# One hybrid decoder block on one core: other loads, roots and order in the first stage

## The chip, the cores and the metric

The kernel runs on one core of a Trainium2 chip. TensorE multiplies and transposes, VectorE and ScalarE do elementwise work, GpSimd (POOL) and SyncE (SP) here only issue DMAs. The metric is the device time in microseconds of one execution of the whole program, the median of several runs. Data begin and end in device memory.

## The reference, cut to what matters

One decoder layer for 512 tokens of width 1024. A conditioning vector `c` gives six modulation vectors; the input is normalized, modulated, and projected; two groups of heads (a gated delta rule, and a native sparse attention) work on the projection, an output projection and a gated MLP with a short convolution follow.

```python
mod = jax.nn.silu(c) @ ada_w + ada_b
shift1, scale1, gate1, shift2, scale2, gate2 = jnp.split(mod[:, None, :], 6, axis=-1)
h = rmsnorm(x, norm1_w) * (1 + scale1) + shift1
proj = h @ w_in
... # gated delta heads and sparse attention heads on proj -> mixed
x = x + gate1 * (mixed @ w_out)
h2 = rmsnorm(x, norm2_w) * (1 + scale2) + shift2
up = causal_dwconv(h2 @ ffn_w_up, ffn_conv_w, ffn_conv_b)
a, b = jnp.split(up, 2, axis=-1)
x = x + gate2 * ((jax.nn.silu(a) * b) @ ffn_w_down)
```

Here `rmsnorm(x, w) = x * rsqrt(mean(x*x) + 1e-6) * w`. All inputs are float32.

## The kernel before, in words

**Arithmetic.** A float32 product is made of three products of rounded parts (`mm3`): every operand is split into `hi` (rounded, by ScalarE or VectorE) and `lo = src - hi` (VectorE), and `hi*hi`, `hi*lo`, `lo*hi` are accumulated in a PSUM bank. So each weight tile costs one rounding and one subtraction before TensorE can use it.

**First stage.** `x` is loaded as eight tiles of 128 tokens by 512 features (256 KB each), `xs[t][j]`. For each token block `t`, both halves are squared and summed (`square2`, on ScalarE or VectorE), `rsqrt1` makes the reciprocal root on VectorE, and `scale` multiplies the tiles by it. The root starts from a bit trick and refines it in three steps of two operations each; `rsqrt` is the same for several columns, with three operations in each step.

The width of 1024 is worked through in eight steps `k` of 128 features. Step `k` needs
- the modulation of its 128 features: `mod_scale(k, 0, ...)` and `mod_shift(k, 1)`. For most of them two tiles of `ada_w` (`adat`, 128 x 512, 256 KB) are loaded and VectorE reduces each against `cb`, the row of `silu(c)` broadcast over all partitions (`mod`, a `scalar_tensor_tensor` with `accum_out`). `cb` is made by eight TensorE products of `sc = silu(c)` with the identity. Only the scale of `k = 0` is made otherwise: from `adat0`, by eight products of one column on TensorE;
- the transposes of the four `xs` columns (TensorE, with `ident`), `Identity` with scale and bias on ScalarE into `h`, and the split of `h` into `hTh[k]`, `hTl[k]`;
- the weights `wg0[k]` (128 x 896, 448 KB) and their split.

Then 7 x 3 products go into seven PSUM banks `g0` (`g0_first` for `k = 0`, in two halves of 256 columns; `g0_mm` for the others, 512 columns).

**Warm-up.** At the start TensorE is given `IDLE = 64` products of a blank tile (`128x256`), sect "warm"; nothing uses them. ScalarE is given one Silu of a blank column.

**Later stages.** Seven projections in this first pass, then convolutions, the delta rule in four chunks of tokens, the sparse attention, the output projection, a second norm (`norm2`, with `rsqrt1`), the up-projection by a seven-product scheme, and the down-projection. `rsqrt` is called for the norm of k and q (32 columns), and through `rms` in the four scans, for `nq`, `kv` and `cmp`.

**What sets the order.** Every operation is recorded into a plan and then emitted in an order that is written out as packed text: `ORDER` holds the differences of operation numbers, `CHOICE` says for each operation that ScalarE or VectorE could do which of the two does it. Each engine does its instructions in the order of emission, and so does each DMA queue. Since the plan emits everything from one place, all instructions have the same line, L262, in the profile.

DMAs are issued by SP (hardware queue), some by GpSimd (software queue). Before the first real product SP issues, in this order: x[0,0], x[0,1], x[1,1], x[1,0], ident, x[2,0], x[3,1], x[3,0], x[2,1], shift k=0 (second half), `adat0` (first half), `wg0[0]`, `adat0` (second half), shift k=0 (first half), then tiles for k = 1 and 2. GpSimd loads the first 48 columns of the parameters `pt` (`c`, norm weights, modulation biases).

TensorE's first instructions are: 29 fillers; the eight products for `cb`; then the other 35 fillers, one to seven at a time, between the transposes for k = 0, 1, 2 and the eight products for the scale of k = 0; then the 42 products of `g0_first`.

Of the kernel before, what the change touches and what calls it, by code (L numbers as in the profile page):

```python
# [12 lines left out]
IDLE = 64  # L13
F32R = mybir.dt.float32r
I32 = mybir.dt.int32
AF = mybir.ActivationFunctionType
# [5 lines left out]
P = 128  # L22
# [12 lines left out]

GQ, GK, GV, GZ = 0, 512, 1024, 1536
# [9 lines left out]
def _fill(table, fields):  # L46
    at = 0
    for name, n in fields:
# [7 lines left out]
                   ("alog", 4), ("dtb", 4), ("w2k", 128), ("w2v", 128)])  # L56
NCST = _fill(CST, [("triu", 128), ("ones", 128), ("negT", 128), ("neg", 128), ("eye2", 512), ("lv", 2 * 128),
# [5 lines left out]
c-ozNcbF8#7wx@0Gn-gg1PPLJ1_>fTa?VJWAUPvBD@l?l8Ob@S2#A0Z6iE^U6a++amaydDF1tI^_r6m#1H$`$@1MthGt*sNU0rqS+;h*ZYNF^)cuWFQBqfG7  # L63
N!XxGi7ASn>sRWb59o>hq5=Jol9Xwkw!v>WMNp!qrdzrJW&eMFxkJC(RJ9(Z!BI-OU|UOu&u_1_JAe|<ht!k-eR`}1aqTEg*RNlz)09lV&F8AR`ZnFw=Q@@K
Xma}Z<>!hPp$B^0-q(drpez%4Fuvq;1|J{BzY*6O<NLplhwf=lI-vVCKb^(Z?Br?~WkU;3RP>%c(p|6gV=z9I=tq5~wP-W!6hi^6PpeVGiz~}*&7oABe$v|X
2d?L(E%;7{r<kWXcve~pqi~G#n&zbK7>!>qs$X-X>;~@kQ8bQDY7Tsxc`$#;@Qgn-FOJI4JlvIrp6XRtsSQd*PwIR4J{_uS{tDpEWc0Uf&GhOQ?S$t&*C-qh
(n)xJyq-e+Y^Zxyv!FB$J=8>f0~QS6u5$FJcBJ{}>3OY0SF`{u;iCM$W~F~%lVrd~tiFYI%xI5k4SYY-Cwdz-O-XXPj9xOXUqu^JXt2hssgaHHV@?=X(_+4j
h40{w9J+?e;`ydVG1%!3U@|p&P=<bnz1~3|0~$lY-k-<Jc<ghd(B}x0-T`V#(mu3!OW(w}BPkzU0)}EWAD)qeZllH%{RlHu0Bu$ygZLU2mGyB~0Xn5+QJ<+9
uz61_((mZ&8?cWLcTS+WdKpM#%#o>6-{SWlJIA&8n*5`M(PkK3Q}0WBq=NNtqQ*5Xh5p5apG$~DkIj|d_#KTaqv%`u(U&igG3L~${n)m*B&=EDEzO7-JENu8
FQ)8*j-f2DVPn(?S~mE74(B<^%)(Hd&9jz6?XWzF0gQD;So_5ExH>8<SJE%KTp#FD%*JKSY&|}LTGQuL(vHKAe#gR&Yjluy3tOJpo(9qz8cT)sB!#Jmztgsu  # L70
oxezdiZq&m4jXLgX<({|e!*4Y*YD~kZ_Yq2ji&Wsd$d$yWy*|sn8JQ<@1%GY@o+)?8-2{KS7`$k@~q?Z{w{h<+5$C2FxI8&b0R(K{k6HGObu(BC|UydKc%C-
?ujw*mCV$IPXM7MsFQrb4($cjr%1W5J&C>fg7;Zcq_3|351k`ZdAy9%%2bzrz$|W|k8~fuD+Q?@SE1dSLo0>VPHfJTr6xU6<4?)a_EjKkwtmj*q*vJD#FgF+
flRbQ9_l-^9+)V{F}|lsc_;_P$sRqd4LJwRk!Jj@T)~X@2s@D2f-eIpm$W*KlW-cv`@C=aSIb&0i5dNvQ_)yS2Hbe4EFYJ&bW|Jh_fiheuF2m>0`9!3*L4)1
1UF8XOz`ORoD=h#0KSR#txdeC=_w;$l=V8CZ%VPSZHe!29w6ej+{C>Kd}iY^;JOQXPBJ@<ou&Rf9H+%KANP~FVevXKu>^}YpxfRI{!{SPqrhrB=CPt4@wrL2
# [12 lines left out]
u1f_`J<5$}lq}*Y+Lxa23fDvBCEW452e>R+`3VsrH%G&7t4Kx4>|ArFdj<rIHp}c(lJ45Z^G)C$rGht=qhB@BTRN~0-Z73x$x+W6lsn)DYZS%V0mN?6Ce9;w
vge&Z1u&0lBO0iMoxjnS!p=mUB>VJ$r(D2ClfZSgXqZ&wL$Lh&Gy)Osu;-fQ3Va7#`M{Yz+QK!(Xw6OB2nZ~J=zfwq=|tz5OcbN%R5y6kU5IPuNe^|pb4MD>
c_+VH&Uxxa&=77WMRDz8{MJOwUnoB#3YeT>hekN7v^nnF#J|E1_sNGq&{nVwL#^}#lWx*FxcVzvJS_b=8wK2NxDA+fAWcJ^L3p0(HfZdA)SI(Oewysmcau9A
i3L%C6R4KEmn+L&Rw(u?VwCX5P!mk|_%2wyvMh8uxei^zy?=9gF=KfETn%s{;im)L^`0gH)y|$<vd2x-i<}2ssL(crJ*xwS5gAWuLB#xDxr2U6Z_q4i1Py&3  # L90
sEDLyati$`962wcyu@*|Z01s^e+h9qnFO_D_s9kDw>YCjI$>lm65&+UZDL}-YM7JgMmW#i^?2q;8RE3kx5aUCU`$Cm2$=9W0nK3Bsl(ePAD@xbxXa{13Un0V
Q&NbpB2sMQOVUKA>2&m`A6JCxO^5h(iR(*k^rIcL%E!C`a~w(ibhw_Uyqcd6%SbTx+rac(8m5ad(<!JT?ShRzL&=En!-+BOG}tpcqGzOZ=R&kne&qwmnW{mn
pFpfUuQ!lw{jFc~b6qGYk$p|p*>r$rxleT$SCzV+t$_pFSG({e-K-sf)w$^Xd-6M%5OU6IK1t;yxn?B4!>e-2Wj1=YE~%Rc?>J`FZAFykMaE#X@?|yINB}uk
F7(>fLU?vGa<_emXIW_vdRB&7(E~XP+-&5Q93iKvC{OpcO)#D-oC!L-zpr>wektl4(9*~jdO&ICgkAmxQ+x26fLTc)shz!AL;eI$^rdRr3K*;4Iqp8Ax9MXY
s44j@lz|8S5w7>8lttz$egw<^gS_D>tdbuX@k<1!;f+#M-$E?kOZ8yuqH-Q6%BrimAXwvfEvfO8&#4c+v4tGDB)8?$@FfY|JhSy)pscsPZVuG*{1OPTM=oe@
k3+Kp88NH3z))?%a|94kba3EHPw7B3m(<^>uQMS~+DXz_x2xwTssn2W^s=mWM|c|0@IY11C*Z{*G~3_L`zMqXQzoZ1r=^mC3f|E=4Ez;vw|gQeoj#!Qfiq58
V9rHMi=aV>)Y<e7b)y*BL8;sV-UY}-ys*Y;;K{EW;obFRAm)1!mksRqc&TjQj;9Kp@fYwm1?O}F>SLTzwAg>pvl1<y<a~ix9S84hOJBI7Jj>-GxHJcPGa)e4
f$HNrR887C2eqDlE9cz8j)$(mZ?bwTB5%2?(*r5J@nHXG>B^r3(s^ruDQ5*HdKOqeNuYayEKUQ=M;dvqP)u%irxwj|b2}~{^EYr(LCr-&0bSK++*Hm(4bG8#
# [1347 lines left out]
```

## Time and profile before

| | |
|---|---|
| median of 3 runs | 653.7 us (653.41 to 654.44) |
| the profiled execution: its own time | 654.27 us |
| its span, first to last instruction | 652.4 us |
| instructions | 12661 |
| TensorE products busy | 647.6 us |
| TensorE weight loads busy | 584.1 us |
| VectorE busy | 613.4 us |
| ScalarE busy | 467.9 us |
| moved by DMA | 132.44 MB |

In rows of the profile PE is TensorE's products, PEld its weight loads, DVE VectorE, ACT ScalarE, SPq the DMA issues of SP. Tiles are named by their class: S, R, s and C are SBUF pools (512 columns, 1024 columns, small, kept), P is PSUM; `in_adat_dram` stands for both `adat` and `adat0`, `in_wg_dram` for `wg0`. Times in a timeline are start and duration in us, `x4` counts instructions merged into the row, and brackets give the idle time of the engine before it and what ended it. A float32 product that is not split shows as two instructions.

### The profile page before, as it was taken

Reading aid. Unit: us, or ns where it says so; the run is one execution under the profiler, and the core shown is the slowest. Engines: PE = TensorE matmul, PEld = TensorE weight load, DVE = VectorE, ACT = ScalarE, POOL = GpSimd, SP = SyncE. Lnnn points to the kernel's source line nnn. Section 1 sums busy time; section 2 is a strip of 40 time slices with the busy share of each in tenths; the row PEclk is TensorE's granted clock in tenths of the full one; section 3 lists DMA queues with packets and bytes.
Section 4 is the critical chain, followed back from the end, with each engine's and each line's share of the span. In section 5 each row is a group of like instructions: output and inputs, shape, how many; then the busy total and the mean of one; then the engine's idle time right before and its main releaser. Section 6 shows DMA issues by size and latency. Waiting matters only on the chain.

```text
span 652.4 us, 12661 instructions
## 1 busy us (share of the span) xinstructions
PE 647.6 (99%) x4167; PEld 584.1 (90%) x4167; DVE 613.4 (94%) x1531; ACT 467.9 (72%) x1165; POOL 136.3 (21%) x160
## 2 busy tenths in 40 slices
PE   9999999999999999999999999999999999999997
PEld 9887878888988889988899999999999998888886
DVE  6999989896899999989999999999989999999998
ACT  6668977245768999927775665766677899998850
POOL 0000100010100003321222523334233431343500
PEclk9999999999999999999999999999999999999999
DMA  8999673585614499994878999999999999999923
GB/s 316 393 344 318 211 216 90 178 193 131 178 28 167 134 324 238 225 264 120 182 172 199 170 177 190 214 228 192 199 233 210 203 228 270 275 183 201 151 42 130
DMA packets 71771, 132.44 MB, mean 203 GB/s; under 512 B 15588, under 2 KB 16276, under 8 KB 71704
## 3 DMA queue, kind: packets, MB, share of 16 engines
q1 hardware_dynamic: 49480, 91.46, 42.2%
q0 software_dynamic: 22224, 40.16, 37.9%
q8 instruction: 33, 0.54, 0.3%
q14 instruction: 34, 0.28, 0.1%
HBM read 109.56 MB, written 3.41 MB: 173 GB/s over the span
## 4 chain that ended last, share of the span: by engine, by line
PE 95%; DMA 3%; DVE 1%; SPq 0%; issue 0%
PE P L262 95%; DMA S<-in_adat_dram 2%; DVE S L262 1%; DMA S<-in_x_dram 1%; SPq L262 0%; DVE C L262 0%; DVE s L262 0%
## 5 line engine op out<-in xcount | busy, mean ns | idle before, releaser
L262 PE MATMUL P<-S,S 128*128 128x256 f32 (+3 forms) x3675 | 602.9, 323 | 0.1
L262 PEld LDWEIGHTS P<-S,S 128*128 128x128 f32 (+1 forms) x3675 | 524.6, 190 | 53.2 <-ACT S L262 1.0
L262 DVE TENSOR_TENSOR S<-S,S 128x512 fp32r<-128x512 f32 (+12 forms) x470 | 234.7, 539 | 6.7 <-ACT S L262 2.5
L262 ACT ACTIVATE S<-S 128x512 fp32r<-128x512 f32 (+3 forms) x364 | 180.9, 548 | 50.9 <-DVE S L262 32.1
L262 ACT ACTIVATE S<-P 128x256 f32<-128x256 f32 (+6 forms) x212 | 83.0, 415 | 55.3 <-PE P L262 54.0
L262 ACT ACTIVATE S<-R 128x512 fp32r<-128x512 f32 (+2 forms) x153 | 85.0, 582 | 27.2 <-PE P L262 7.6
L262 POOL DMA_DIRECT2D S<-R x46 | 43.1, 1028 | 261.8 <-PE P L262 83.2
L262 POOL DMA_DIRECT2D S<-in_wu_dram x66 | 62.4, 1026 | 143.3 <-DVE S L262 95.6
L262 DVE SCALAR_TENSOR_TENSOR S<-S,C,S 128x511 f32<-128x511 f32 (+2 forms) x116 | 84.5, 742 | 0.7 <-ACT S L262 0.6
L262 DVE TENSOR_TENSOR S<-P,S 128x256 f32<-128x256 f32 (+4 forms) x125 | 65.3, 531 | 11.8 <-PE P L262 9.8
L262 DVE TENSOR_TENSOR S<-R,S 128x512 fp32r<-128x512 f32 (+2 forms) x100 | 56.8, 585 | 0.4 <-ACT S L262 0.2
L262 ACT ACTIVATE S<-S,C 128x512 f32<-128x512 f32 (+1 forms) x60 | 41.6, 701 | 13.5 <-DVE S L262 7.2
L262 PE MATMUL P<-C,S 128*128 128x128 f32 (+3 forms) x285 | 49.5, 269 | 0.0
L262 DVE SCALAR_TENSOR_TENSOR S<-S,S 128x512 f32<-128x512 f32 x62 | 41.1, 682 | 0.9 <-DMA S<-in_adat_dram 0.8
L262 PEld LDWEIGHTS P<-C,S 128*128 128x128 f32 (+1 forms) x285 | 36.0, 146 | 6.5 <-ACT S L262 1.1
L262 POOL DMA_DIRECT2D S<-S x26 | 22.1, 864 | 68.3 <-ACT S L262 63.5
L262 ACT ACTIVATE S<-S,s 128x128 f32<-128x128 f32 (+4 forms) x77 | 34.7, 478 | 1.3 <-DVE s L262 1.2
L262 ACT ACTIVATE S<-P,C 128x128 f32<-128x128 f32 (+1 forms) x72 | 26.8, 436 | 7.8 <-PE P L262 7.5
L262 DVE SCALAR_TENSOR_TENSOR S<-P,C,S 128x511 f32<-128x511 f32 (+3 forms) x48 | 29.3, 643 | 0.8 <-ACT S L262 0.6
L262 ACT ACTIVATE S<-P,C,C 128x128 f32<-128x128 f32 (+2 forms) x36 | 16.8, 527 | 9.8 <-DVE C L262 5.5
L262 DVE TENSOR_TENSOR S<-S,P 128x256 f32<-128x256 f32 (+1 forms) x39 | 18.5, 475 | 1.1 <-PE P L262 0.8
L262 PE MATMUL P<-S 128*128 128x256 f32 (+1 forms) x96 | 17.6, 330 | 1.2 <-DVE S L262 1.2
(79 smaller groups left out, 293.3 us busy)
## 6 DMA issues: line engine op xcount, KB each, us to landing
S<-in_wu_dram POOLq DMA_DIRECT2D x66, 256.0 KB, 5.7
S<-in_adat_dram SPq DMA_DIRECT2D x64, 256.0 KB
S<-R POOLq DMA_DIRECT2D x46, 256.0 KB, 5.7
S<-in_wu_dram SPq DMA_DIRECT2D x44, 256.0 KB
R<-in_wu_dram SPq DMA_DIRECT2D x22, 512.0 KB
S<-in_wd_dram SPq DMA_DIRECT2D x44, 256.0 KB
S<-in_adag_dram SPq DMA_DIRECT2D x32, 256.0 KB
R<-in_wn_dram SPq DMA_DIRECT2D x12, 512.0 KB
```

The costliest lines, as they stand in the source:

```text
L262: getattr(engines[eng], method)(*map(place, args), **{k: place(v) for k, v in kw.items()})
```

## The change

- The identity and the first 48 parameter columns come as one tensor, `first` (128 x 176, 88 KB), by one DMA on SP; GpSimd's load of the 48 columns is gone. The other parameters come later into a smaller `pt`.
- x[0,1] is issued by ScalarE's queue, the first thing in ScalarE's order; the other seven tiles by SP.
- The shift of k = 0 is made like its scale: `adat0` holds both, and eight more products of one column on TensorE replace two reductions on VectorE.
- The roots: two steps, the first of third order, the second of second order, on inputs scaled by `RS*RS`. `rsqrt1` has seven operations instead of eight (four calls in the first stage, four in `norm2`), `rsqrt` eight instead of ten (eight calls).
- `IDLE` is 22 instead of 64.
- `ORDER` and `CHOICE` are new texts. The order differs on every engine from the start into the up-projection; 107 of the operations that two engines can do change engine. The last 593 operations of TensorE stand as before.

The new first stage, read from the text: SP issues x[0,0], `first`, x[1,0], x[1,1], x[3,1], x[3,0], `adat0` shift (two halves), x[2,0], x[2,1], `adat0` scale (two halves), `wg0[0]`, then shift and scale tiles of k = 1 around `wg0[1]`, the four modulation tiles of k = 2, two of k = 3, `wg0[2]`, and so on (before, `wg0[2]` came ahead of the last tile of k = 2). TensorE gets 13 fillers; the eight products for `cb`; one filler; three transposes; four fillers; the eight products of the shift with a transpose among them; four fillers; the eight products of the scale; eight transposes; then `g0_first`. ScalarE: the DMA issue, the square of x[0,1], Silu of `c`, squares of x[1,0], x[1,1], x[3,1], x[3,0], the copies of `cb`, scalings, the rounding of the first 512 columns of `wg0[0]`, then `Identity` and rounding for k = 0. The Silu of the blank column stands 54th. VectorE: the work on x, the sum for the shift, the rounding of the last 384 columns of `wg0[0]`, the two sums for the scale, then subtractions and the reductions of k = 1.

```diff
-IDLE = 64
+IDLE = 22
+RS = 1024.0 / 27.0
+MAGIC = float(0x5F3759DF - (1 << 31))
+NP0 = 48
...
 def rsqrt(v, n, y):
-        V.tensor_scalar(y.bitcast(I32), v.bitcast(I32), -0.5, float(0x5F3759DF), op0=OP.mult, op1=OP.add)
-        for _ in range(3):
-            V.scalar_tensor_tensor(a, y, -0.5, y, op0=OP.mult, op1=OP.mult)
-            V.tensor_mul(a, a, v)
-            V.scalar_tensor_tensor(y, a, 1.5, y, op0=OP.add, op1=OP.mult)
+        V.tensor_scalar(y.bitcast(I32), v.bitcast(I32), -0.5, MAGIC, op0=OP.mult, op1=OP.add)
+        V.tensor_mul(b, y, v)
+        V.tensor_mul(a, b, y)
+        V.scalar_tensor_tensor(b, a, -10.0 / 3.0, a, op0=OP.add, op1=OP.mult)
+        V.scalar_tensor_tensor(y, b, 5.0, y, op0=OP.add, op1=OP.mult)
+        V.tensor_mul(b, y, v)
+        V.tensor_mul(a, b, y)
+        V.scalar_tensor_tensor(y, a, -64.0 / 3.0, y, op0=OP.add, op1=OP.mult)
...
-    G.dma_start(pt[:, :48], par[:, :48])
...
-            Q.dma_start(xs[t][j], x[t, j])
-    Q.dma_start(ident, ide)
+            (S if (t, j) == (0, 1) else Q).dma_start(xs[t][j], x[t, j])
+    Q.dma_start(first, ide)
...
 def rsqrt1(ss):
-        for _ in range(3):
-            V.scalar_tensor_tensor(a, y, v[:, 0:1], y, op0=OP.mult, op1=OP.mult)
-            V.scalar_tensor_tensor(y, a, 1.5, y, op0=OP.subtract, op1=OP.mult)
+        V.scalar_tensor_tensor(a, y, v[:, 0:1], y, op0=OP.mult, op1=OP.mult)
+        V.scalar_tensor_tensor(b, a, -10.0 / 3.0, a, op0=OP.add, op1=OP.mult)
+        V.scalar_tensor_tensor(y, b, 5.0, y, op0=OP.add, op1=OP.mult)
+        V.scalar_tensor_tensor(a, y, v[:, 0:1], y, op0=OP.mult, op1=OP.mult)
+        V.scalar_tensor_tensor(y, a, -64.0 / 3.0, y, op0=OP.add, op1=OP.mult)
...
+    def mod0(i):
+        part = bank("part")
+        for j in range(2):
+            raw = u("ada0", shape=(P, 4, P))
+            Q.dma_start(raw, adat0[i, j])
+            for a in range(4):
+                kk = j * 4 + a
+                T.matmul(part[:, j:j + 1], raw[:, a, :], sc[:, kk:kk + 1], start=a == 0, stop=a == 3)
+        return part
...
     def mod_shift(k, i):
-        part = mod(k, i)
+        part = mod0(i) if i == 1 and k == 0 else mod(k, i)
```

More of the change, by code (lines that the diff above doesn't have):

```diff
@@ L363, in square @@
         S.activation(junk, src, AF.Square, accum_out=acc)
-    pt, ident = keep("pt", NPAR), keep("ident", P)
+    pt, first = keep("pt", NPAR - NP0), keep("first", P + NP0)
+    ident = first[:, :P]
     ct = [u("ct") for _ in range(3)]
-    G.dma_start(pt[:, :48], par[:, :48])
     def pr(name, a=0, n=None):
         at, m = PAR[name]
-        return pt[:, at + a:at + a + (m - a if n is None else n)]
+        tl, at = (first, at + P) if at < NP0 else (pt, at - NP0)
+        return tl[:, at + a:at + a + (m - a if n is None else n)]
     def cs(name, a=0, n=None):
@@ L408, in square2 @@
         junk = u("sq")
-        plan.either(("activation", (junk, src, AF.Square), dict(scale=(2 * D) ** -0.5, accum_out=acc)),
-                    ("scalar_tensor_tensor", (junk, src, 0.5 / D, src), dict(op0=OP.mult, op1=OP.mult, accum_out=acc)))
+        plan.either(("activation", (junk, src, AF.Square), dict(scale=RS * D ** -0.5, accum_out=acc)),
+                    ("scalar_tensor_tensor", (junk, src, RS * RS / D, src), dict(op0=OP.mult, op1=OP.mult, accum_out=acc)))
     def rsqrt1(ss):
         v, y = small("v1", 1), small("y1", 1)
-        V.scalar_tensor_tensor(v, ss[:, 0:1], EPS / 2, ss[:, 1:2], op0=OP.add, op1=OP.add)
-        V.tensor_scalar(y.bitcast(I32), v.bitcast(I32), -0.5, float(0x5F3759DF - 0x400000 - (1 << 31)),
-                        op0=OP.mult, op1=OP.add)
-        a = small("a", 1)
-        for _ in range(3):
-            V.scalar_tensor_tensor(a, y, v[:, 0:1], y, op0=OP.mult, op1=OP.mult)
-            V.scalar_tensor_tensor(y, a, 1.5, y, op0=OP.subtract, op1=OP.mult)
+        a, b = small("a", 1), small("b", 1)
+        V.scalar_tensor_tensor(v, ss[:, 0:1], RS * RS * EPS, ss[:, 1:2], op0=OP.add, op1=OP.add)
+        V.tensor_scalar(y.bitcast(I32), v.bitcast(I32), -0.5, MAGIC, op0=OP.mult, op1=OP.add)
+        V.scalar_tensor_tensor(a, y, v[:, 0:1], y, op0=OP.mult, op1=OP.mult)
[3 more added lines that the diff above has]
+        V.scalar_tensor_tensor(y, a, -64.0 / 3.0, y, op0=OP.add, op1=OP.mult)
         return y
@@ L444, in mod @@
         return part
-    def mod_scale(k, i, norm, dst):
-        if i == 0 and k == 0:
-            part = bank("part")
-            for j in range(2):
-                raw = u("ada0", shape=(P, 4, P))
-                Q.dma_start(raw, adat0[j])
-                for a in range(4):
-                    kk = j * 4 + a
-                    T.matmul(part[:, j:j + 1], raw[:, a, :], sc[:, kk:kk + 1], start=a == 0, stop=a == 3)
-        else:
-            part = mod(k, i)
+    def mod0(i):
[7 more added lines that the diff above has]
+        return part
+    def mod_scale(k, i, norm, dst):
+        part = mod0(i) if i == k == 0 else mod(k, i)
         t_ = small("t", 1)
@@ L461, in mod_shift @@
     def mod_shift(k, i):
-        part = mod(k, i)
+        part = mod0(i) if i == 1 and k == 0 else mod(k, i)
         V.scalar_tensor_tensor(modc[:, i * 8 + k:i * 8 + k + 1], part[:, 0:1], part[:, 1:2], adab[:, i, k:k + 1],
@@ L507, in hybrid_block @@
     g0_mm(KT - 1)
-    Q.dma_start(pt[:, 48:], par[:, 48:])
+    Q.dma_start(pt, par[:, NP0:])
     for i, c in enumerate(ct):
@@ L1405, in _layout @@
     adat = f(np.stack([aw[:, a:a + D].reshape(2, 512, KT, P).transpose(2, 0, 3, 1) for a in (1024, 0, 4096, 3072)]))
-    adat0 = f(aw[:, D:D + P].reshape(2, 4, P, P).transpose(0, 2, 1, 3))
+    adat0 = f(np.stack([aw[:, a:a + P].reshape(2, 4, P, P).transpose(0, 2, 1, 3) for a in (D, 0)]))
     ada1 = f(np.stack([ab[2048:3072], ab[5120:6144]]))
```

222 lines of the change are left out of this document (114 added, 108 removed).

## The prediction

> **What bounds the kernel now.** I read the page first (engines, chain), then the chain in order of time, then the timeline of the first 28 us instruction by instruction, then waits and windows for the rest.
>
> ```profile
> span 652.4 us, 12661 instructions
> PE 647.6 (99%) x4167; PEld 584.1 (90%) x4167; DVE 613.4 (94%) x1531; ACT 467.9 (72%) x1165; POOL 136.3 (21%) x160
> ```
> ```profile
> 14.80 7.82 DMA S<-in_adat_dram
> ...
> 24.92 620.64 PE P L262 x3982
> ```
> TensorE is busy all the time, and from 24.92 us the chain is nothing but TensorE. The end is therefore the moment at which the real products start, plus a fixed amount of them, plus TensorE's stalls. Only the start and the stalls can move, and both lie in the first stage. Windows of the rest (columns: PE, PEld, DVE, ACT, POOL busy; clock; DMA share; GB/s):
>
> ```profile
> 2.00:7.00 5.00, 5.00 (x25) 5.00 (x25) 1.69 (x7) 1.25 (x6) 0.00 (x0) 1.00 0.94 292
> ...
> 28.00:50.00 22.00, 22.00 (x107) 17.86 (x107) 21.89 (x67) 13.92 (x24) 0.00 (x0) 1.00 0.96 357
> 60.00:150.00 90.00, 90.00 (x447) 73.71 (x446) 85.36 (x239) 57.09 (x163) 5.58 (x7) 1.00 0.68 187
> 150.00:290.00 140.00, 140.00 (x916) 125.18 (x915) 127.45 (x414) 113.76 (x384) 18.55 (x21) 1.00 0.67 186
> ```
> TensorE is full in each, VectorE has some slack after 60 us and next to none at 28 to 50 us. Now the start. SP's queue, the waits that show what its issues wait for, and the last links before the first real product:
>
> ```profile
> 6.13 0.33 SPq L262 DMA_DIRECT2D S<-in_adat_dram  x1
> 6.79 0.33 SPq L262 DMA_DIRECT2D R<-in_wg_dram  x1
> ...
> 10.97 0.33 SPq L262 DMA_DIRECT2D S<-in_adat_dram  x1
> ...
> 12.78 0.33 SPq L262 DMA_DIRECT2D R<-in_wg_dram  x1
> 13.45 0.33 SPq L262 DMA_DIRECT2D S<-in_adat_dram  x1
> ```
> ```profile
> 6.13 0.69 DVE L262 SCALAR_TENSOR_TENSOR S<-S 128x512 f32<-128x512 f32 x1 [1.13 <-DMA S<-in_x_dram]
> ...
> 6.80 0.63 ACT L262 ACTIVATE S<-S 128x512 f32<-128x512 f32 x1 [1.89 <-DMA S<-in_x_dram]
> ...
> 12.12 0.63 ACT L262 ACTIVATE S<-R 128x512 fp32r<-128x512 f32 x1
> 12.22 0.35 DVE L262 CAST S<-R 128x384 fp32r<-128x384 f32 x1
> ...
> 14.09 0.55 PE L262 MATMUL P<-C,S 128*128 128x1 f32 x4
> 14.41 0.22 DVE L262 SCALAR_TENSOR_TENSOR s<-P,C 128x1 f32<-128x1 f32 x1 [0.23 <-PE P L262]
> 14.55 0.28 DVE L262 SCALAR_TENSOR_TENSOR C<-s,C 128x1 f32<-128x1 f32 x2
> 14.92 0.57 ACT L262 ACTIVATE S<-P,C,C 128x256 f32<-128x256 f32 x1 [0.41 <-DVE C L262]
> 15.52 0.42 ACT L262 ACTIVATE S<-S 128x256 fp32r<-128x256 f32 x1
> ...
> 16.21 1.00 PE L262 MATMUL P<-S,S 128*128 128x256 f32 x7
> ```
> By the order, SP's 11th and 12th issues are those at 6.13 and 6.79, and the third and fourth x tiles' users start at the same moments: eight loads are in flight, and the n-th issue marks the landing of load n-8. So load 11 had landed by 10.97 us, load 13 (`adat0`'s second half, the last input of the first scale) at 12.78 us, load 14 at 13.45 us. The scale's last products, spread among fillers, end after 14.4 us; then come the two small sums, `Identity`, the rounding, and at 16.21 us the first real product.
>
> Once it runs, TensorE stalls on VectorE and ScalarE, and VectorE had waited for a shift tile:
>
> ```profile
> 22.64 0.69 DVE L262 SCALAR_TENSOR_TENSOR S<-S,S 128x512 f32<-128x512 f32 x1 [0.77 <-DMA S<-in_adat_dram]
> ...
> 24.92 0.19 PEld L262 LDWEIGHTS P<-S,S 128*128 128x128 f32 x1 [0.50 <-DVE S L262]
> 25.38 1.70 PEld L262 LDWEIGHTS P<-S,S 128*128 128x128 f32 x8 [0.28 <-ACT S L262]
> ```
>
> **The change part by part.**
>
> *Loads ahead of the first product.* The new order needs x, `first`, four `adat0` tiles and `wg0[0]` before it: 8 x 256 + 88 + 4 x 256 + 448 KB, 14 loads on two queues. The old kernel's first 14 on SP, with the small parameter load on POOL, are the same kinds: 8 x 256 + 64 + 24 + 4 x 256 + 448 KB. To the KB it is the same, so I take load 14's 13.45 us for the landing of `wg0[0]`, which now comes last; the scale's last tile lands one load (448 KB, about 1.1 us at some 400 KB/us: two 256 KB landings are 0.67 us apart) earlier, near 12.3 us. Its four products are eight instructions on one column; four took 0.55 us from the first start to the last end, so 1.1 us at most, and they are done when the weights land.
>
> *x by ScalarE's queue.* At 2 to 7 us the DMA engines are already 0.94 busy with one queue feeding them. One issue fewer on SP gives at most the 0.33 us that an issue takes, at least nothing, below that a loss if ScalarE's table load stands in front of its issue (1.28 us, row below); that loss falls on x[0], which is needed late. I take 0. Dropping POOL's load frees POOL, which has nothing to do then: 0. Behind the wait of Silu for `first` stand ScalarE's squares of x, idle in front of them before (1.89 us): 0.
>
> *From landing to product.* In the new order VectorE's cast of the last 384 columns of `wg0[0]` (0.35) stands before the two small sums. From the first sum to `Identity` were 0.51 us, with one operation of the shift between, 0.13 us by the pair's rows, that now stands earlier: 0.38. So `Identity` could start at 13.45 + 0.35 + 0.38 = 14.18 us; ScalarE's own rounding of the weights, before it in its order, ends at 13.45 + 0.63 = 14.08 and does not hold it up. From `Identity` to the product were 1.29 us (16.21 - 14.92). First real product: 15.47 us, **0.74 us earlier**. Bounds: none if `wg0[0]` lands one 256 KB load (0.67 us) later, 1.1 with the 0.33 us of the queue.
>
> *First shift by products.* VectorE loses two reductions on 512 columns; TensorE gets eight products of one column, 16 instructions, at most four times 0.55 us, while it waits for loads: 0 there, up to 2.2 us if that cover were gone.
>
> ```profile
> L262 DVE SCALAR_TENSOR_TENSOR S<-S,S 128x512 f32<-128x512 f32 x4 | 2.7, 686 | 0.1
> L262 DVE SCALAR_TENSOR_TENSOR s<-s,s 128x1 f32<-128x1 f32 x24 | 3.6, 185 | 0.2
> ```
> *Roots.* `rsqrt1` loses one of eight operations (3.6 / 24 = 0.15 us), `rsqrt` two of ten. In the first stage that is 4 x 0.15 = 0.6 us, with 2 x 0.69 for the shift and one square of x given to ScalarE (0.69): 2.7 us of VectorE's work less before about 28 us. Part of it becomes waiting for loads, since VectorE now idles until 13.45.
>
> *The stalls.* The four modulation tiles of k = 2 now come before that step's 448 KB of weights, not behind them: about 1.1 us earlier, more than the 0.77 us that VectorE waited, and VectorE has less to do. Both stalls at 25 us should go; 0.50 + 0.28 us on the weight loads, of which I take **0.6**, since the product in flight covers some. Bounds 0 and 0.78. What is late next is ScalarE's rounding of the next step, by about as much as TensorE itself.
>
> *The rest.* All later roots (8 x 2 and 4 x 1 operations of 0.15 us, 3 us on VectorE) lie under a full TensorE: 0. The order changes far into the up-projection; what it can give is bounded by the waits that are left after 60 us:
>
> ```profile
> PEld P L262 <- ACT S L262: 1.7, 8, 0.3
> PEld P L262 <- issue: 1.6, 6, 0.4
> PEld P L262 <- DVE C L262: 0.4, 1, 0.4
> ```
> 1.7 + 0.4 = 2.1 us at most (nothing else changes for "issue"), and as much could come back where orders moved. I take 0.
>
> Sum: 0.74 + 0.6 = 1.3 us. The profiled execution took 654.27 us, 0.6 above the median; it goes to 652.9, so the median of 653.7 goes to **652.4 us**.
>
> **The rivals.**
>
> *The clock of TensorE is not up when the products start (slower).* The kernel issues 22 fillers instead of 64.
>
> ```profile
> 1.20:6.60 5.40, 5.40 (x25) 5.40 (x26) 1.84 (x6) 1.85 (x5) 0.70 (x1) 1.00 0.85 257
> ...
> 16.30:20.30 4.00, 4.00 (x36) 4.00 (x35) 4.00 (x16) 2.81 (x6) 0.00 (x0) 1.00 1.04 392
> ...
> 648.90:651.90 3.00, 0.00 (x0) 0.00 (x0) 0.81 (x2) 0.00 (x0) 0.00 (x0) 1.00 0.69 254
> 651.90:652.40 0.50, 0.00 (x0) 0.00 (x0) 0.00 (x0) 0.00 (x0) 0.00 (x0) 0.62 0.00 0
> ```
> ```profile
> 0.74 1.28 ACT L262 ACT_TABLE_LOAD   x1 [0.74 <-PEq L1436]
> 1.19 6.24 PE L262 MATMUL P<-S 128*128 128x256 f32 x29 [1.19 <-DVE S L262]
> ```
> The same 256 columns take 0.21 us each before 6.6 us (25 in 5.40) and about 0.115 after 16 us (35 starts in 4.00), though the clock column says 1.00 for both; and the last rows show the granted clock falling about 3 us after the last product. So TensorE starts slow, needs about 5.5 us of unbroken work (1.2 to 6.7) to become fast, and loses it after 3 us without work. The new order has 13 fillers in a row, 13 x 0.21 = 2.8 us to 4.0 us, then waits for `first` and Silu. The old first ScalarE operation, a Silu on a blank column, is moved behind some 50 others, so the load of its table may stand between the first square and the Silu of c, another 1.28 us of pause. After that only nine fillers break the waits. Against it: no pause reaches 3 us. Price: 5.5 us from 15.5 us at 0.21 are 26 products that take 26 x 0.115 = 3.0 us when fast: 2.5 us lost, 1.3 gained, 1.2 us slower: 654.9 us; with a second such stretch up to 657. It decides from 1.3 / (1 - 0.115/0.21) = 2.9 us of slow products.
> The Trainium skill (TensorE: Matmul & The Clock Gate, "What's actually happening") says that the clock is halved by default and released only after a busy window of about 3.4 us, of windows that run freely. The rows agree on the two speeds and on the fall at the end. By that rule 2.8 us of fillers fill no window and the products start slow; an estimate from that page of one to two windows, 3.4 to 6.8 us, would cost 1.5 to 3.1 us, and the time would be about 653.9 to 655.5.
>
> *The gain is eaten (no change).* VectorE is 21.89 of 22 us busy at 28 to 50 us. If it sets the pace there, TensorE arrives earlier only to wait, and the time stays at 653.7 (653.3 to 654.1). Against it: it has 2.7 us less to do.
>
> *More waits go than I count (faster).* If the waits after 60 us go too, 652.4 - 2.1: about 650.5.
>
> **How the numbers follow.** A measurement tells about 0.2%, 1.3 us. Forecast 0.48: its sum lies at that edge, and its upper bounds (1.1 + 0.78 us) reach further than its doubts on the late side, so 0.32 faster and 0.16 same. More waits gone 0.10, faster. Eaten 0.18, same. Slow clock 0.24, of which 0.02 within 1.3 us and 0.22 slower. Together 0.42, 0.36, 0.22. The range leaves out half of "more" and the worst of the slow clock: 650.9 to 655.3. The forecast's own range is 651.6 to 653.2.
>
> **What would show it.** First product on 256 columns of real data near 15.5 us and its successors 0.115 us apart; if they are 0.21 apart, the clock was it. No wait of TensorE over 0.3 us at 20 to 28 us. A square and then a second table load before 8 us on ScalarE would lengthen the pause between the fillers and the broadcast of c. New waits of TensorE on VectorE at 28 to 60 us would show the gain eaten. Wrong altogether would be a later landing of `wg0[0]` than 14.2 us, or TensorE waits after 60 us that differ by more than 1 us.

## The result, and the profile after

The changed kernel takes **658.4 us** (median of 6 runs, 657.49 to 660.95) against 653.85 us before (6 runs): ratio 1.0076, 95% interval 1.0054 to 1.0097, **slower by 0.8%**. The forecast was 652.4 us. The profiled execution took 657.61 us (before: 654.27), 0.8 us under its median; the runs lie 3.5 us apart, those of the kernel before 1.0 us.

The page's first lines after the change:

```profile
span 655.5 us, 12556 instructions
...
PE 646.5 (99%) x4141; PEld 583.0 (89%) x4141; DVE 611.3 (93%) x1504; ACT 469.3 (72%) x1165; POOL 134.0 (20%) x159
```

TensorE is busy 1.1 us less than before, and the span is 3.1 us longer: TensorE starts its real work later or stops more. The chain of work that ended last says where (start, duration, what):

```profile
0.74 3.64 DMA S<-in_x_dram
...
4.40 0.72 ACT S L272 x2
...
5.14 1.28 ACT L272
...
6.44 0.22 ACT C L272
...
6.70 8.40 PE P L272 x61
...
15.12 0.24 DVE s L272
...
16.70 377.13 PE P L272 x2325
...
394.34 8.06 DMA R<-in_wu_dram
...
406.87 241.38 PE P L272 x1612
```

Before, TensorE came on this chain only at 24.92 us and stayed on it unbroken. Now the chain runs through ScalarE (a second table load, 1.28 us, then Silu of `c`), then 8.40 us of TensorE without a wait, and there is a new break near 400 us. TensorE's timeline of the first stage, the two waits of ScalarE and VectorE in it, and the stretches between edges of the granted clock (columns of windows as in the prediction; the 1.00 of the first row is no record: the first record begins at 9.68 us, and the products for `cb` in that row are 0.21 us apart):

```profile
1.19 3.14 PE L272 MATMUL P<-S 128*128 128x256 f32 x13 [1.19 <-DVE S L272]
6.70 3.46 PE L272 MATMUL P<-C,C 128*128 128x128 f32 x16 [2.37 <-ACT C L272]
...
10.92 1.90 PE L272 MATMUL P<-C,S 128*128 128x1 f32 x17
12.68 0.72 PE L272 MATMUL P<-S 128*128 128x256 f32 x4
13.24 2.77 PE L272 MATMUL P<-C,S 128*128 128x1 f32 x24
16.70 4.54 PE L272 MATMUL P<-S,S 128*128 128x256 f32 x24 [0.69 <-ACT S L272]
```
```profile
1.18 1.28 ACT L272 ACT_TABLE_LOAD   x1 [1.18 <-PEq L1452]
...
5.14 1.28 ACT L272 ACT_TABLE_LOAD   x1
6.44 0.21 ACT L272 ACTIVATE C<-C 128x8 f32<-128x8 f32 x1
```
```profile
15.12 0.22 DVE L272 SCALAR_TENSOR_TENSOR s<-P,C 128x1 f32<-128x1 f32 x1 [1.15 <-PE P L272]
```
```profile
6.27:9.67 3.40, 2.97 (x14) 2.97 (x15) 2.24 (x14) 2.88 (x10) 0.00 (x0) 1.00 1.05 381
9.69:13.09 3.40, 3.40 (x32) 3.40 (x32) 2.63 (x15) 2.89 (x8) 0.00 (x0) 1.00 1.04 401
13.10:16.50 3.40, 2.91 (x27) 2.67 (x25) 2.18 (x9) 2.34 (x5) 0.00 (x0) 1.00 1.05 397
16.51:19.91 3.40, 3.21 (x15) 3.21 (x16) 3.40 (x14) 1.95 (x5) 0.00 (x0) 0.50 1.08 394
19.93:23.33 3.40, 3.40 (x30) 3.40 (x30) 3.40 (x14) 3.14 (x5) 0.00 (x0) 1.00 1.03 389
```

The first real product comes at 16.70 us, 0.5 us later than before, and the first 15 products run at a granted clock of 0.50, 0.21 us each. Matching TensorE's instructions from the end, each against the one that stands as many from the end in the kernel before, gives how late it is (us, worked out from the traces; time is that of the kernel before; where the orders differ the two are not the same product, which leaves some hundredths uncertain):

| at | 20.8 | 29.7 | 125 | 270 | 290 | 409 | end of TensorE |
|---|---|---|---|---|---|---|---|
| changed kernel | +1.99 | +0.90 | +1.19 | +1.02 | +1.38 | +2.64 | +2.68 |

So: 2.0 us lost by 20 us, 1.1 us won back by 30 us (where the kernel before stalls; a part of that comes of being late, see below), 0.4 us lost near 274 and 1.3 us near 406 us. The rest of the 3.3 us lies behind TensorE's end: 0.4 to the end of the span and 0.2 outside it.

### The profile page after: what moved, and what is told of

Its sections match the earlier page's. It is cut to its first block, busy times and chain, and to the rows that moved or that the text cites. A ratio compares the mean times of both kernels' runs of the same rounds, so it can differ in the third digit from the quotient of the medians.

```text
span 655.5 us, 12556 instructions
## 1 busy us (share of the span) xinstructions
PE 646.5 (99%) x4141; PEld 583.0 (89%) x4141; DVE 611.3 (93%) x1504; ACT 469.3 (72%) x1165; POOL 134.0 (20%) x159
## 3 DMA queue, kind: packets, MB, share of 16 engines
HBM read 109.56 MB, written 3.41 MB: 172 GB/s over the span
## 4 chain that ended last, share of the span: by engine, by line
PE 96%; DMA 2%; DVE 1%; ACT 1%; issue 0%; SPq 0%; ACTq 0%; DVEq 0%
PE P L272 96%; DMA R<-in_wu_dram 1%; DVE S L272 1%; DMA S<-in_x_dram 1%; ACT S L272 0%; ACT L272 0%; SPq L272 0%; DVE s L272 0%; ACT C L272 0%; DVE C L272 0%; ACTq L272 0%; DVEq L272 0%
## 5 line engine op out<-in xcount | busy, mean ns | idle before, releaser
L272 DVE TENSOR_TENSOR S<-S,S 128x512 fp32r<-128x512 f32 (+11 forms) x470 | 235.2, 545 | 5.3 <-ACT S L272 1.3
L272 ACT ACTIVATE S<-S 128x512 fp32r<-128x512 f32 (+3 forms) x369 | 183.9, 549 | 46.0 <-DVE S L272 26.6
L272 ACT ACTIVATE S<-P 128x256 f32<-128x256 f32 (+5 forms) x207 | 82.3, 416 | 58.4 <-PE P L272 48.8
L272 ACT ACTIVATE S<-R 128x512 fp32r<-128x512 f32 (+1 forms) x154 | 85.4, 582 | 17.0 <-DMA R<-in_wu_dram 8.0
L272 POOL DMA_DIRECT2D S<-in_wu_dram x66 | 60.7, 1003 | 137.5 <-DVE S L272 103.9
L272 PE MATMUL P<-C,S 128*128 128x128 f32 (+2 forms) x301 | 49.9, 270 | 0.0
L272 PEld LDWEIGHTS P<-C,S 128*128 128x128 f32 x301 | 36.6, 148 | 5.9 <-ACT S L272 1.5
L272 ACT ACTIVATE S<-S,s 128x128 f32<-128x128 f32 (+4 forms) x72 | 33.3, 485 | 0.8 <-DVE s L272 0.7
L272 PE MATMUL P<-R,S 128*128 128x512 f32 (+2 forms) x72 | 18.9, 368 | 0.0
```

The costliest lines, as they stand in the source:

```text
L272: getattr(engines[eng], method)(*map(place, args), **{k: place(v) for k, v in kw.items()})
```

## The experiments

Three theories: the **clock** (TensorE's clock falls, and the first real products are slow); the **start** (TensorE's own row of 8.40 us, begun late by the table load, is the path); the **later order** (new waits far from the first stage). A rival to each is that loads set the pace and nothing of it matters. Every ratio is to the kernel before, run beside; its medians were 653.7 to 653.9 us.

### Is it the clock?

Each run has a mean granted clock over its span, and it tells how often the clock fell: one stretch of 3.41 us at half clock takes 0.0026 off a mean over 652 us, so 0.997 is one such stretch and 0.995 two. The time before the clock first rises is not in it.

**The old kernel with 22 fillers**, its order otherwise as it was:

```diff
-IDLE = 64     # 29 at the front, 35 between the first stage's products
+IDLE = 22     # 13 at the front, 1 + 4 + 4 between
```


> The kernel before, its order as it was, with 22 fillers instead of 64: the first 13, one behind the products for cb, four ahead of the first product of the scale, four behind the last one. Theory 'clock': nothing that TensorE needs comes later, but its clock is not up when the real products start at 16.2 us: 14 to 28 of them at 0.21 instead of 0.117 us, 1.4 to 2.8 us, so 655.2 to 656.6 us against 653.8. Rival 'the fillers do nothing, the rest of the new order is what costs': 653.8 within 0.3.

655.40 us (653.63 to 657.26, 12 runs), 1.0022 [1.0012, 1.0032], where the runs of the unchanged kernel beside it stay within 1.2 us. The missing fillers alone cost 1.7 us, and one and the same program now varies by 3.6 us. Eight of the 12 runs have a mean clock of 0.994 to 0.997; the slowest has 1.000, so falls after the first rise are not all of it. By the matching above the kernel is 2.47 us late at 20.8 us and 1.85 us at 29.7 us: with the old order and the old code 0.6 us come back there merely because TensorE is late.

**The changed kernel with 12 more fillers at the front** (13 + 12, in the pause up to 6.70 us).

> The changed kernel with 12 more fillers behind its first 13, which fill TensorE's pause from 3.92 to 6.7 us and delay nothing. Theory 'clock, lost by the early pause': the clock is up by 6.9 us, the 16 product instructions for cb take 0.117 instead of 0.214 us each (1.6 us less), the first real product comes at about 15.1 us, its successors are 0.117 us apart, and the time is about 658.4 - 1.6 - 1.5 = 655.3 us. Theory 'clock, lost in the sparse stretch from 13 to 16.5 us': the products for cb become fast, but some 14 of the first real products still take 0.21 us: about 656.8. Rival 'clock matters nothing': 658.4.

656.38 us (654.45 to 657.86), 1.0039 [1.0023, 1.0054]: two of six runs kept a clock of 1.00 (655.37 and 654.45 us), the others did not. In the profiled run the clock was up early, and the first product came at 15.20 us, as expected, 1.0 us ahead of the kernel before. That both stretches count, the early pause and the sparse one, fits this, but the traces of the other four runs are not kept.

**36 fillers, spread among the one-column products, and the Silu of the blank column early** (F is a filler, T a transpose, and the others stand for eight products each; the lines put the order into words):

```diff
-13 F | cb | F | 3 T | 4 F | shift | 4 F | scale | 8 T
+18 F | cb | F | 3 T | 4 F | shift with 2 F | 4 F | scale with 2 F | 8 T with 5 F
```


> The changed kernel with ScalarE's Silu of the blank column early again and 36 fillers instead of 22, put where TensorE waits or has room: 18 ahead of the products for cb, two among the shift's products, two among the scale's, five among and behind the last transposes. Theory 'clock': the runs, which spread over 3.5 us in the changed kernel, draw together to about 1 us as before; the first real product comes at about 15.2 us and nothing real takes 0.21 us; what is left is the gain of the start (about 0.9 us at 100 to 290 us, as in the one run of the kernel with more fillers that had no slow stretch) and the late stall (0.8 to 1.4 us): 653.3 to 654.2 us. Rival 'one-column products keep the clock down whatever stands between them': spread and median as with the early Silu alone, 656.8.

658.09 us (657.13 to 658.88), 1.0066 [1.0054, 1.0078]: the miss. No run kept its clock, and by the matching above it lost 1.7 us near 274 and 1.3 us near 406 us. The rival was nearer: fillers in ones and twos between one-column products do not hold the clock.

What does? Between any two edges of the granted clock, 3.41 us apart, I counted TensorE's instructions in the traces: wide ones (256 columns, or 128 of an unsplit product or transpose, all 0.107 to 0.12 us apart at full clock) and those of one column.

| stretches at full clock, after which it | wide + one-column instructions |
|---|---|
| fell (9 stretches) | 5+27, 7+20, 8+21, 9+13, 9+14, 9+16, 9+20, 10+15, 10+22 |
| held (the lowest) | 12+17, 12+19, 14+16, 15+0, 16+4, 16+15, 17+0, 17+12 |

In every kept trace ten wide instructions or fewer: it falls, whatever else runs. Twelve or more: it holds. One-column instructions count for nothing, although they keep TensorE as busy in the profile (0.112 us each): the stretch with 15 wide ones and nothing else, 2.36 us busy, held, and one with 9+20 and no pause at all fell. So the products were **made wide**, at the same number and the same 0.112 us:

```diff
-                T.matmul(part[:, j:j + 1], raw[:, a, :], sc[:, kk:kk + 1], start=a == 0, stop=a == 3)
-        return part
+                T.matmul(part[:, j * P:j * P + P], raw[:, a, :], sc[:, kk:kk + 1].to_broadcast([P, P]),
+                         start=a == 0, stop=a == 3)
+        return part[:, :2 * P].rearrange("p (j n) -> p j n", j=2)[:, :, 0]
```


> The changed kernel with one edit: the 16 products of one column (scale and shift of k = 0) are made with sc's column repeated 128 times, so each instruction streams 128 columns instead of one; only the first column of the result is used. At full clock such an instruction takes 0.112 us either way (the products for cb have that shape). Theory 'a stretch of 3.41 us with fewer than some 12 wide instructions drops the clock': from 10 us on every such stretch has 20 or more, so no real product takes 0.21 us; the start stays near 16.7 us, because the products for cb still wait for the second table load and run at half clock. Time 658.4 - 1.5 = about 656.9 us, a little less where runs had two slow stretches. Rival 'it is the pauses of TensorE that drop the clock, not the width': 658.4 and up to 3.5 us of spread as in the changed kernel.

656.46 us (655.74 to 658.13, 5 runs), 1.0043 [1.003, 1.0056]: 1.9 us off, somewhat more than the theory has it. In the profile the clock rises once and stays, but only at 12.03 us, and that run is the slowest of the five; two of the others have a mean clock of 0.996 and 0.997, so a stretch fell in them all the same. Where, no kept trace shows. The opposite edit, one-column products put back into the repaired kernel described below (653.11 us):

> The kernel with early Silu, 18 leading fillers and the new order in the first stage only, with the one-column products of the change in place of the wide ones. Theory 'one-column products let the clock fall': in most runs a stretch of 3.41 us holds fewer than 11 wide instructions and the clock falls for the next: median 1.5 to 2.5 us above the kernel with wide products (654.6 to 655.6 us), runs 3 us apart, the fastest of them at 653.1 us. Rival 'the width does nothing once the first fillers stand': 653.1 and within 1 us of each other.

654.80 us (652.90 to 655.58, 11 runs), 1.0011 [1.0002, 1.002], **1.7 us slower than with wide products**. All 11 runs have a mean clock of 0.993 to 0.997, all 11 of the wide kernel 0.999 or 1.000. The three at 0.997, one stretch, took 652.90 to 653.49 us; the eight with more lost took 654.58 to 655.58. The two profiles side by side, the narrow kernel's stretches first, then the wide one's over the same times:

```profile
6.90:10.29 3.39, 3.29 (x29) 3.08 (x29) 2.58 (x17) 2.63 (x9) 0.00 (x0) 1.00 0.95 341
10.31:13.70 3.39, 3.32 (x29) 3.11 (x29) 2.48 (x14) 2.99 (x7) 0.00 (x0) 1.00 1.05 409
13.73:17.12 3.39, 3.18 (x16) 2.78 (x15) 3.36 (x11) 3.33 (x8) 0.00 (x0) 0.50 1.05 397
```
```profile
6.90:10.29 3.39, 3.03 (x27) 2.83 (x26) 2.43 (x16) 2.92 (x9) 0.00 (x0) 1.00 1.03 387
10.31:13.70 3.39, 3.25 (x29) 3.05 (x28) 2.87 (x16) 2.97 (x8) 0.00 (x0) 1.00 1.05 406
13.73:17.12 3.39, 2.58 (x22) 2.34 (x21) 3.39 (x10) 2.94 (x7) 0.00 (x0) 1.00 1.04 391
```

In the middle stretch both have 29 instructions on TensorE, 3.32 and 3.25 us of it busy; one loses its clock for the next 3.41 us, the other doesn't. The busy column can't tell them apart, the tile shapes can. (The wide kernel's own stretches have other edges, 7.89, 11.30 and 14.72 us; each of them has 22 wide instructions or more.) The narrow run shown is one of the three that lost a single stretch: it is 1.2 us behind the wide one at 20.8 us, 0.2 us at 29.7 us, and ends at 653.49 against 653.41 us. One stretch costs next to nothing here; the 1.7 us come from the runs that lost more.

### What sets the start?

**Early Silu alone**: in ScalarE's order the Silu of the blank column stands behind the issue of x[0,1], not 54th.

> The changed kernel with one operation moved: ScalarE's Silu of the blank column stands second in ScalarE's order, behind the issue of x[0,1], not 54th. Theory 'TensorE is the path of the start' (from the Silu of c to the first sum TensorE works 8.4 us without waiting): the second table load of 1.28 us goes, the products for cb start at 5.4 instead of 6.70 us, the first real product at 15.4 instead of 16.70 us, and the median of 658.4 us falls by 1.3 to about 657.1 us; with the slow clock gone too it would be 655.7. Rival 'loads set the start': the first real product stays within 0.3 us of 16.7 us and the time at 658.4.

656.77 us (656.53 to 659.07), 1.0053 [1.0041, 1.0066]: 1.6 us off. The products for `cb` started at 5.18 us as expected, but in the profiled run the clock fell early, over the scale's products, and the first real product came at 16.89 us. The same edit undone in the repaired kernel, where the clock holds:

> The kernel with wide products, 18 leading fillers and the new order in the first stage only, but with the Silu of the blank column 54th on ScalarE, as the change has it, so that a second table load stands between the first square and the Silu of c. Theory 'TensorE has about as much room as the table load takes': the products for cb start at 6.4 instead of 5.1 us, TensorE is ready for the first sum at 13.5 instead of 12.9 us, where VectorE needs it at 13.3: 0.1 to 0.4 us slower in most runs, 653.2 to 653.5 us, and 1.5 us more in the runs whose clock comes up only after the pause. Rival 'the 1.28 us count in full': 654.4.

653.75 us (653.45 to 654.82), 1.0003 [0.9995, 1.0012]: 0.64 us above 653.11, half of the load's 1.28, a little more than expected. (The two profiled runs, 653.45 and 653.41 us, do not show it, though the first product comes at 15.35 against 14.95 us.)

**Is a load by ScalarE's queue worth anything?** In the repaired kernel, x[0,1] issued third by SP:

```diff
-            (S if (t, j) == (0, 1) else Q).dma_start(xs[t][j], x[t, j])
+            Q.dma_start(xs[t][j], x[t, j])
```


> As the kernel with the new order in the first stage only, but x[0,1] is issued by SP, third in its order, not by ScalarE's queue. Theory 'a second hardware queue costs about 0.2 us outside the span': time minus span is 1.8 us, as before the change, not 2.0, and one more issue on SP moves the first product by 0.3 us at most: within 0.2 us of that kernel, either way. Rival 'the second queue brings the first loads earlier': the first real product comes 0.4 us later or more.

654.50 us (653.66 to 655.06), 1.0007 [0.9998, 1.0016], **1.4 us slower** than the repaired kernel. The theory fell (time less span stays at 1.8 us in both), the rival held, by more than it said. The first user of x[0,1], TensorE's wait for the first tile of the shift and the first real product, x by SP first, then the repaired kernel:

```profile
5.45 0.63 ACT L260 ACTIVATE S<-S 128x512 f32<-128x512 f32 x1 [3.21 <-DMA S<-in_x_dram]
...
9.78 2.16 PE L260 MATMUL P<-C,S 128*128 128x128 f32 x17 [0.48 <-DMA S<-in_adat_dram]
...
16.20 8.04 PE L260 MATMUL P<-S,S 128*128 128x256 f32 x54 [0.82 <-ACT S L260]
```
```profile
4.22 0.63 ACT L260 ACTIVATE S<-S 128x512 f32<-128x512 f32 x1 [1.56 <-DMA S<-in_x_dram]
...
8.43 2.16 PE L260 MATMUL P<-C,S 128*128 128x128 f32 x17 [0.36 <-DMA S<-in_adat_dram]
...
14.95 6.90 PE L260 MATMUL P<-S,S 128*128 128x256 f32 x49 [0.81 <-ACT S L260]
```

The tile lands 1.23 us earlier (it is issued at 0.73, not at 1.66 us), and so the square, Silu of `c` and the products for `cb` start earlier. But it is not that row which sets the first product: behind it TensorE waits for a tile of `adat0` in both kernels, and VectorE begins the square of the last x tile, behind a wait for it, at 10.51 instead of 11.77 us. So the later loads come earlier too, and the first product with them, by 1.25 us. SP issues the first `adat0` tile only 0.5 us earlier (3.54 against 4.03 us); why the loads land more than that earlier stays open. In the two profiled runs 0.7 of the 1.25 us are left at the end (654.09 against 653.41 us). Silu of `c` ahead of the square, without a second queue, was not tried.

**Shift of k = 0 on VectorE**, as before the change. A first try with one-column products for the scale and more fillers:

> The kernel with the early Silu, more fillers and the old late order, but with the shift of k = 0 as before the change: two reductions of 512 columns on VectorE, and eight fillers where the eight products stood (42 fillers in all). The first reduction stands in VectorE's pause ahead of the last square of x, the second behind that square. Theory 'VectorE's chain from the last x tile sets the start': the second reduction delays root, scaling and first product by 0.7 us, so it is 0.5 to 0.9 us slower than the same kernel with the products. Rival 'shift by products was free and useless': no difference.

655.04 us (653.57 to 658.20): its clock fell in most runs, so it tells nothing. In the repaired kernel:

> As the kernel with the new order in the first stage only, but with the shift of k = 0 by two reductions on VectorE and eight fillers in the place of its products; the scale's products stay wide, so the clock holds. Theory 'VectorE's chain from the last x tile sets the start': the second reduction, behind the last square, delays the first real product by 0.5 to 0.7 us: 653.1 + 0.6 = 653.7 us. Rival 'no difference': 653.1.

653.48 us (652.94 to 653.87), 0.9991 [0.9982, 1.0], 0.37 us above 653.11, but over the same range (652.95 to 653.83): unclear. The first product came 0.58 us later (15.53 us), as expected; by the matching all of it was won back by 29.7 us (-0.60 at 20.8 and -1.68 there, against -1.18 and -1.33).

**Old roots in `rsqrt1`**, in a kernel with wide products, early Silu and the old order from 300 us on:

> As the kernel with wide products, early Silu and old late order, but rsqrt1 with the old three steps of two operations (eight instead of seven operations; four calls in the first stage, four in the second norm). Theory 'one root stands in the chain from the last x tile to the first product': 0.15 to 0.2 us slower than that kernel. Rival 'VectorE is full there, every operation counts': 0.6 us or more, with stalls of TensorE at 25 to 50 us. Rival 'hidden': no difference.

654.10 us (653.35 to 655.76) against 654.03: no difference. The first product moved by 0.21 us (15.39 against 15.18 us), as the theory has it, and less waiting behind it made up for that.

**The new code in the old order:**

> The new code (one load for identity and early parameters, second on SP; x[0,1] by ScalarE's queue; shift of k = 0 by products; shorter roots) in the old order, with 55 fillers: nine are left out beside the shift's eight products so that TensorE's row stays as long. Theory 'the parts of the code are worth little by themselves, the order made both the gain and the loss': 653.7 within 0.6. Rival 'VectorE's shorter work pays by itself': the stalls of TensorE at 25 us go and the time is 653.1 or less. Rival 'the code parts cost': 654.5 or more, from the shift's last tile, which the old order loads last.

655.86 us (654.95 to 658.17), 1.0042 [1.0026, 1.0057]. Inconclusive on the parts: in its profile 27 one-column and 5 wide instructions fill one stretch, the clock falls, and the first real product comes at 18.45 us.

### What does the later order cost?

**The old order and choice of engines from TensorE's 1700th operation on** (about 300 us), in the changed kernel:

> The changed kernel up to TensorE's 1700th operation (about 300 us), and from there on the order and the choice of engines of the kernel before. Theory 'the new late order costs a stall': TensorE's wait on VectorE near 406 us (1.1 us more than before in that stretch) goes, and the time falls by 1.1 to about 657.3 us, while the first real product stays at 16.7 us. Rival 'TensorE waits as long elsewhere in the old order, behind another first part': 658.4 within 0.4.

655.97 us (654.69 to 658.00), 1.0037 [1.0022, 1.0051]: 2.4 us off, more than the one stall that I had seen, but with a clock that varies. With the fillers of the miss above:

> The kernel of the run before with the old order and choice of engines from TensorE's 1700th operation on. Theory 'two separate losses, clock and late order': both are gone, the time is 653.7 less 0.9 for the start, plus 0.2 for one more queue outside the span: about 653.0 us, and 0.8 to 1.4 us under the kernel with the new late order. Rival 'the late stall depends on when the first stage ends': no difference between the two.

655.82 us (653.82 to 657.24, 12 runs) against 658.09: 2.3 us. And with a steady clock, old late order and new late order:

> The wide products, ScalarE's Silu of the blank column early, 18 instead of 13 fillers ahead of the products for cb, and the old order from TensorE's 1700th operation on. Theory 'clock, second table load and late order are all that the change lost': first real product at 15.2 us, nothing real at 0.21 us, no stall at 406 us, runs within about 1 us of each other, and 653.8 - 0.9 + 0.2 = about 653.0 us, with a small gain over the kernel before. Rival 'something else of the new code costs': 654 or more although the clock holds.

> As the kernel with wide products, early Silu and old late order, but with the new late order, as in the changed kernel. Theory 'the late order costs a stall by itself': 0.8 to 1.5 us slower than that kernel (about 654.2 us), all of it after 400 us. Rival 'the late stall followed from the late first stage': no difference.

**654.03** us (653.57 to 654.58), 1.0003 [0.9994, 1.0012], and **656.12** us (655.22 to 657.64), 1.0039 [1.0025, 1.0052]. The clock holds in both; the late order costs 2.1 us. But the first of them should have been 653.0. Its trace shows where its lead goes, by the same matching as above:

| at | 20.8 | 29.7 | 125 | 270 | 290 | 409 | end of TensorE |
|---|---|---|---|---|---|---|---|
| new late order | -1.11 | -1.34 | -1.11 | -1.19 | -0.04 | +0.77 | +1.03 |
| old order from 300 us | -0.93 | -1.18 | -0.93 | -1.02 | -0.33 | -0.36 | -0.25 |
| old order from 65 us (next) | -1.18 | -1.33 | -1.03 | -1.04 | -0.73 | -0.77 | -0.78 |

Between 270 and 290 us, too, the new order waits. ScalarE and TensorE with the new order there, in the kernel of the miss:

```profile
273.50 1.15 ACT L266 ACTIVATE S<-R 128x512 fp32r<-128x512 f32 x2 [1.36 <-DMA R<-in_wo_dram]
```
```profile
275.18 1.22 PE L266 MATMUL P<-S,S 128*128 128x256 f32 x8 [1.07 <-ACT S L266]
```

ScalarE stands in front of a weight tile of `wo`, and TensorE behind ScalarE. In the kernel of 654.03 us the same two waits are smaller, 0.35 us and 0.26 us on a weight load, and account for some 0.4 of the 0.7 us that it loses there. So the last version takes the new order **only for the first stage**, up to TensorE's 420th operation:

> Wide products, early Silu, 18 leading fillers, and the new order only up to TensorE's 420th operation (about 65 us); from there on the order and choice of engines of the kernel before. Theory 'the rest of the lead is eaten by the new order's wait for a load of wo at 274 us': the wait goes, the lead of 0.9 us lasts to the end, 653.8 - 0.9 + 0.2 = about 653.1 us, and it beats the kernel with the old order from 300 us on (654.0) by 0.6 us or more. Rival 'loads arrive when the DMA engines deliver them, an earlier first stage only waits longer': 653.8 to 654.1, with a wait of TensorE elsewhere.

**653.11 us** (652.95 to 653.83, 11 runs), ratio **0.9987 [0.9979, 0.9996]**, as expected, and faster than both kernels. This is the repaired kernel of the sections above. Its chain is TensorE from 22.16 us to the end (before: from 24.92), and nothing near 274 or 406 us is on it:

```profile
22.16 622.62 PE P L260 x3990
```

From here back to the changed kernel, with medians: +0.92 (new order from 65 to 300 us, 654.03), +2.09 (new late order, 656.12), +1.69 (one-column products, sized in the repaired kernel), +0.64 (late Silu, sized there too): 658.45 us. The changed kernel has 658.37. The last two steps were also measured in the changed kernel itself: late Silu and five fillers fewer, +0.34 (656.46), and one-column products, +1.91 (658.37). Each step is known to about 1 us either way, so the agreement of the sum to 0.1 us is luck.

## Why the prediction was wrong, point by point

- **Landing of the loads: right.** `wg0[0]` was put at 13.45 us; VectorE's cast of it stands at 13.61 us without a wait, so it had landed by then, and by 13.0 us in the repaired kernel.
- **"They are done when the weights land" (16 instructions at 0): wrong, and the first step that failed.** The cover that was named, TensorE's waiting for loads, was not there: TensorE worked from 6.70 to 15.1 us without a wait, and VectorE stood 1.15 us for the scale's products: nearly all of the 1.23 us by which the first product missed 15.47 us. The row was late because it began behind the second table load and because its 16 instructions for `cb` took 3.46 us, against 1.95 before. With the cover gone the text itself had the price: up to 2.2 us.
- **From landing to product (0.74 us earlier): the mechanism was right.** With TensorE in time and the clock up the first real product came at 14.95 to 15.2 us, even ahead of the 15.47 forecast, where VectorE's cast of the weights stood ahead of the forecast's 13.45 us too, at 13.01 us in the repaired kernel.
- **x by ScalarE's queue (0, at most 0.33 us): mis-sized.** It is worth 1.25 us at the first product in the repaired kernel. The price had been taken from one issue alone; that tile is issued 0.93 us earlier, and the later loads landed some 1.3 us earlier too.
- **The second table load**: named only as part of the rival. It came as described, between the first square and Silu, and costs 0.64 us by itself in the repaired kernel. The Trainium skill (ScalarE activation tables: per-element evaluation and per-set limits, "Table sets in the compiler and the runtime") says that the back end places these loads, block by block, for the longest run of functions. The trace does not bear that out here, unless a block ended between the two: one load served Silu and the squares when Silu came first, and two stand in the row when a square does.
- **The stalls at 25 us (0.6): right, with a limit.** The changed kernel's 1.1 us do not show it, since being late wins 0.6 us there by itself. Three kernels whose profiled clock held and whose first product came at 15.35 to 15.53 us (late Silu, old roots, shift on VectorE) do: they won 0.7 to 1.1 us between 20.8 and 29.7 us and were 1.5 to 1.7 us ahead there, against 1.34 us forecast. But kernels that started at 14.95 to 15.2 us won only 0.15 to 0.25 us and were 1.1 to 1.3 us ahead: in the repaired kernel TensorE waits for VectorE at 22.16 us. So a start before about 15.4 us brought nothing more here, and to that extent the rival "the gain is eaten" was right.
- **Roots (0): right**, 654.10 against 654.03 us.
- **The rest (0, within 2.1 us either way): wrong.** 0.9 + 2.1 = 3.0 us of loss. The bound came from the waits of the old order; a new order has waits that the old trace cannot show.
- **The clock, a rival at 0.24: right in sign and near in price, under-rated, and only in part right in mechanism.** TensorE does not need 5.5 us of unbroken work: in one of the traces the clock rises at 4.16 us, 3 us after the first filler. And the counterargument, "no pause reaches 3 us", was the mistake. The longest pause between 9.7 and 16.7 us was under 1 us, and the clock fell all the same: it follows the wide instructions of each 3.41 us, and 16 narrow ones were added where fillers were taken out. Its 2.5 us of loss were 1.7 in the repaired kernel. The Trainium skill (TensorE: Matmul & The Clock Gate, "HAM oscillation — how this bites in real kernels") gives as the rule no gaps of TensorE above some 3.4 us; here that rule is not enough. The same page ("What's actually happening") has windows of 3413 ns that run freely, so that the same kernel differs from run to run: edges that are multiples of 3.413 us apart agree, and so do runs of one kernel that lost one stretch and others that lost two.
- The range ended at 655.3: it held the clock or a loss by the later order, but not both on top of each other.

## What to carry to other kernels

Before fillers are dropped, count TensorE's wide instructions in every 3.4 us up to the real work, not its busy time: here 12 or more held the clock and 10 or fewer lost it, and a one-column product could be made 128 columns wide at no cost in time. When one edit reorders the whole program, take the new order only where the edit works and compare the rest with the old order, because a lead won early can be lost again at the next load that stands in front of an engine. For the first loads of a kernel try a second queue and the right activation table first, and then look at what the earlier start still gains some 10 us later: here a part of it was gone.

## What the hardware showed that was not expected

- The clock of TensorE fell for a stretch of 3.413 us (two in two of nine traces) after a stretch in which the profile shows TensorE 2.73 to 3.41 us busy; 10 wide instructions were too few, 12 enough (11 did not occur).
- A product of one column took 0.112 us per instruction, as one of 128 columns.
- A table load between two functions cost 1.28 us and nothing more (5.14 to 6.44 us).
- One 256 KB tile by a second queue landed 1.23 us earlier than as the third issue of the first queue, where it is issued 0.93 us later.
- Time less span, as a mean over runs, is 1.76 to 1.79 us for the kernels with the old order from 65 us on or throughout, and 1.9 to 2.1 us for those with the new one up to 300 us or further. What lies in that difference stays open.
